# Gathers of the value stages paced two per chunk, their sums two chunks behind on VectorE, and the last mixer's exit to routing tile by tile

## The chip, the cores and the metric

The kernel runs on one core of a Trainium2 chip. The metric is device time in microseconds (us) of one execution, shown as the median of several runs. The engines are called as the profile calls them: PE is TensorE, DVE is VectorE, ACT is ScalarE, POOL is GpSimd, and SP is SyncE, which here only starts transfers.

## The reference, cut to what matters

A trunk of two layers runs over two groups of tokens: a prompt of 128 tokens (tag P) and a sample of 512 tokens (tag S), of 1024 features each, all in float32. Each layer is a mixer (layer 0: Fourier and short convolution; layer 1: an RG-LRU and an RWKV-7 recurrence) followed by PEER, a mixture over 16,384 experts of which each token takes 128 (8 heads of 16).

```
for each layer l:
    h = layer_norm(x) * (1 + sc1) + sh1
    x = layer_norm(ALPHA * x + g1 * (mixer(h) @ w_out))
    h2 = layer_norm(x) * (1 + sc2) + sh2
    # PEER: idx, gate = top 16 of the product keys, per head and token
    act = gelu(sum_d h2[t, d] * u[idx[t, k], d])
    ffn[t] = sum_k gate[t, k] * act[t, k] * v[idx[t, k]]
    x = layer_norm(ALPHA * x + g2 * ffn)
```

## The kernel before, in words

Tokens lie in tiles of 128. PEER is computed in two ways. For three of the four S tiles (`DENSE = (1, 2, 3)`) every expert is computed: `dense_peer` walks over 128 **chunks** of 128 experts. For a chunk, `hidden` multiplies the tokens by the chunk's slice of the table `u` (24 matmuls in a three-term split of float32, `split_matmul`), ACT applies gelu, DVE multiplies by the scattered gates (`ge * gt`, a **product**), ACT and DVE split it into `ah` and `al`, the chunk's slice of `v` is loaded and split into `vh` and `lw`, and 18 matmuls add it to the output. Half of the hidden tiles are computed earlier, in routing, and parked in DRAM (`spill`), so 64 chunks of a layer are light (18 matmuls) and 64 heavy (42). This walk is called the **value stage** here; there is one per layer.

For S tile 0 and for P, which are too small for that, the rows of `u` and `v` are **gathered**: `gather` starts an indirect DMA on POOL that brings one expert's row for each of 128 tokens, 128 x 4 KB, and one DVE instruction uses it (a **sum** below, be it a dot product with `h2` in `dots` or an addition to `acc` in `values`). There are 512 gathers a layer. They are **tasks**: generators in `B.tasks`, of which `B.pump(n)` takes the next n steps. `B.pump` is called from other work: `split` calls it `B.rate` times for each split table block (2 in routing, 0 in the value stage), `one_hot` once, the projections of layer 1's mixer through `B.pace`, and the value stage once per chunk with a share of what is left, `ceil(left / (122 - c))`. In layer 0 the last 88 tasks (`OVER`) are kept for the next mixer. A sum is held back until two more gathers were issued (`defer`, `use_gathered(2)`); gathered rows live in 4 buffers (`GW`), and in the value stage in `B.gb` = 3 more. Table blocks `w` have 3 buffers, and in a pool `B.wb` more.

A scheduler of the framework orders each engine's instructions by program order and by its own estimate of when each is ready; engines then run them strictly in that order. `pace(n, src)` puts a copy of one column of `src` on POOL and ties the next n gathers behind it, so that they start no sooner than `src` is written.

The mixer of layer 1 is a set of generators advanced in turn (`run` in `odd_mixers`): S's recurrence units, P's whole layer behind them, the LRU channels. When all are done, `peer_layer` opens with `end`, the **passage** to routing: the output projection of S (half of it, k = 0 to 3, was added before by `end_early`, so `self.early` is 4), residual, two layer norms, and the transposes into `hi` and `lo`, for two pairs of tiles, each pair loading its four `wout` blocks itself. Then `route` computes queries, scores and top 16, and `scatter_gates` the gates of the dense tiles; meanwhile gathers run.

## Time and profile before

| | us |
|---|---|
| median of 3 runs | 4570.66 |
| lowest and highest of them | 4562.15, 4586.86 |
| profiled execution | 4558.22 |
| its span, first to last instruction | 4556.4 |
| PE busy | 3837.5 (84%) |
| DVE busy | 3467.4 (76%) |
| POOL busy | 1387.9 (30%) |
| DMA moved | 1198 MB, 263 GB/s over the span |

The table's second part is from the profile page; the DMA engines' mean share and the granted PE clock are also given by stretch. A row of the view by stretches reads: start and end in us from the span's start, length, busy time of PE, PEld (weight loads), DVE, ACT and POOL with the number of instructions in brackets, granted PE clock as a share of 2.4 GHz, mean share of the 16 DMA engines, GB/s. The stretches used are: end of layer 0's routing (780 to 1024), layer 0's value stage (1024 to 1911, cut at 1545 where its gathers end), mixer of layer 1 (1911 to 2958), passage (2958 to 3088), routing of layer 1 (3088 to 3640), its value stage (3640 to 4532, cut at 4282 where the gathers end), and a tail of 24 us.

### The profile page before, as it was taken

Reading aid. Unit: us, or ns where it says so; the run is one execution under the profiler, and the core shown is the slowest. Engines: PE = TensorE matmul, PEld = TensorE weight load, DVE = VectorE, ACT = ScalarE, POOL = GpSimd, SP = SyncE. Lnnn points to the kernel's source line nnn. Section 1 sums busy time; section 2 is a strip of 40 time slices with the busy share of each in tenths; the row PEclk is TensorE's granted clock in tenths of the full one; section 3 lists DMA queues with packets and bytes.
Section 4 is the critical chain, followed back from the end, with each engine's and each line's share of the span. In section 5 each row is a group of like instructions: output and inputs, shape, how many; then the busy total and the mean of one; then the engine's idle time right before and its main releaser. Section 6 shows DMA issues by size and latency. Waiting matters only on the chain. (4 is left out here: it accounts for less than half of the span.)

```text
span 4556.4 us, 71571 instructions
## 1 busy us (share of the span) xinstructions
PE 3837.5 (84%) x26326; PEld 3142.3 (69%) x26326; DVE 3467.4 (76%) x7480; ACT 1757.4 (39%) x3391; POOL 1387.9 (30%) x1105
## 2 busy tenths in 40 slices
PE   7977968999888999778889877719779888988897
PEld 4653767997766788634665654508779877877786
DVE  3398999987889744668554786589999787888845
ACT  2211235763322333244575543203357623332332
POOL 0044322434556200044000232253125354466300
PEclk9997989999999999887888877759999999999999
DMA  9699856999999755368531566487569999999853
GB/s 342 227 350 356 264 196 236 349 357 355 360 360 362 280 175 172 128 237 286 177 101 58 182 222 205 169 289 248 171 225 341 346 367 342 346 365 369 310 170 120
DMA packets 455551, 1198.05 MB, mean 263 GB/s; under 512 B 52848, under 2 KB 195312, under 8 KB 452128
## 3 DMA queue, kind: packets, MB, share of 16 engines
q1 hardware_dynamic: 307744, 656.54, 41.4%
q0 software_dynamic: 147456, 536.94, 32.8%
q8 instruction: 207, 3.39, 0.3%
q14 instruction: 144, 1.18, 0.1%
HBM read 1093.34 MB, written 99.98 MB: 262 GB/s over the span
## 5 line engine op out<-in xcount | busy, mean ns | idle before, releaser
L1079 PE MATMUL ps<-hiS,lwS 128*128 128x384 f32 (+1 forms) x2304 | 817.5, 356 | 81.2 <-DVE lwS L1224 80.9
L1079 PE MATMUL ps<-loS,uhS 128*128 128x384 f32 (+1 forms) x2432 | 857.9, 353 | 1.1 <-DVE loS L432 1.1
L1079 PE MATMUL ps<-hiS,uhS 128*128 128x384 f32 (+1 forms) x2304 | 813.2, 353 | 51.3 <-ACT geS L1252 26.0
L1079 PEld LDWEIGHTS ps<-hiS,lwS 128*128 128x128 f32 x2304 | 447.2, 194 | 111.7 <-DVE lwS L1224 101.4
L1222 ACT ACTIVATE uhS<-w 128x1024 fp32r<-128x1024 f32 x304 | 320.8, 1055 | 527.3 <-PE ps L1079 358.6
L1285 PE MATMUL ps<-vh,ah 128*128 128x512 f32 x1536 | 429.4, 401 | 99.9 <-ACT vh L1222 78.8
L1152 POOL DMA_INDIRECT g<-v,idxP x256 | 351.7, 1374 | 515.8 <-DVE h2P L1168 311.9
L1152 POOL DMA_INDIRECT g<-u,idxS x256 | 349.0, 1363 | 512.9 <-DVE g L1138 391.9
L1079 PEld LDWEIGHTS ps<-hiS,uhS 128*128 128x128 f32 x2304 | 447.5, 194 | 82.3 <-ACT uhS L1222 34.1
L1285 PE MATMUL ps<-lwS,ah 128*128 128x512 f32 x1536 | 483.4, 396 | 10.9 <-DVE lwS L1224 10.8
L1079 PEld LDWEIGHTS ps<-loS,uhS 128*128 128x128 f32 x2432 | 471.5, 194 | 24.0 <-DVE loS L432 3.7
L1285 PE MATMUL ps<-vh,al 128*128 128x512 f32 x1536 | 477.3, 393 | 0.0
L1224 DVE TENSOR_TENSOR lwS<-w,uhS 128x1024 fp32r<-128x1024 f32 x304 | 369.7, 1217 | 122.9 <-ACT uhS L1222 82.0
L1152 POOL DMA_INDIRECT g<-v,idxS x256 | 367.8, 1437 | 237.6 <-DVE h2S L1168 178.6
L1224 DVE TENSOR_TENSOR lwS<-w,vh 128x1024 fp32r<-128x1024 f32 x256 | 312.9, 1223 | 153.7 <-issue 79.3
L1152 POOL DMA_INDIRECT g<-u,idxP x256 | 291.7, 1139 | 414.2 <-DVE g L1138 183.2
L1285 PEld LDWEIGHTS ps<-vh,ah 128*128 128x128 f32 x1536 | 289.1, 192 | 167.1 <-ACT vh L1222 92.5
L1278 ACT ACTIVATE ah<-geS 128x384 fp32r<-128x384 f32 x256 | 134.3, 525 | 671.4 <-PE ps L1285 598.9
L1138 DVE SCALAR_TENSOR_TENSOR g<-g,h2P 128x1024 f32<-128x1024 f32 x256 | 310.2, 1216 | 81.4 <-DMA g<-u,idxP 81.0
L1168 DVE SCALAR_TENSOR_TENSOR h2P<-g,wtP,h2P 128x1024 f32<-128x1024 f32 x254 | 324.6, 1278 | 50.7 <-DMA g<-v,idxP 49.2
L1285 PEld LDWEIGHTS ps<-lwS,ah 128*128 128x128 f32 x1536 | 291.2, 191 | 81.6 <-DVE lwS L1224 20.1
L1285 PEld LDWEIGHTS ps<-vh,al 128*128 128x128 f32 x1536 | 291.4, 190 | 62.8
(480 smaller groups left out, 6687.9 us busy)
## 6 DMA issues: line engine op xcount, KB each, us to landing
w<-ut SPq DMA_DIRECT2D x256, 512.0 KB
w<-v SPq DMA_DIRECT2D x256, 512.0 KB
w<-wblk SPq DMA_DIRECT2D x142, 512.0 KB
w<-wmod SPq DMA_DIRECT2D x96, 512.0 KB
gt<-G SPq DMA_DIRECT2D x64, 768.0 KB
w<-wout SPq DMA_DIRECT2D x56, 512.0 KB
ged<-geS SPq DMA_DIRECT2D x128, 192.0 KB
G<-fa SPq DMA_DIRECT2D x12, 2048.0 KB
```

Of the source, the lines that this page charges most:

```text
L1079: self.nc.tensor.matmul(out, a[:, s], b[:, k, :], start=k == 0 and i == 0, stop=k == 7 and i == 2)
L1138: self.nc.vector.scalar_tensor_tensor(u, u, 1.0, self.h2[t], OP.mult, OP.mult, accum_out=self.act[t][:, s:s + 1])
L1152: self.nc.gpsimd.indirect_dma_start(out=g, out_offset=None, in_=self.I[tab], in_offset=bass.IndirectOffsetOnAxis(ap=self.idx[t][:, s:s + 1 ...
L1168: nc.vector.scalar_tensor_tensor(acc, v, w[:, s:s + 1], acc, OP.mult, OP.add)
L1222: self.nc.scalar.activation(h, raw, AF.Copy)
L1224: self.nc.vector.tensor_tensor(lo, raw, h.bitcast(F32), op=OP.subtract)
L1278: nc.scalar.activation(ah, ge, AF.Copy)
L1285: nc.tensor.matmul(outs[n][h], a[:, s], b[:, 512 * h:512 * h + 512], start=c == 0 and i == 0, stop=c == 127 and i == 2)
```

## The change

In the value stage, each chunk now paces its gathers behind its own product: `pace(min(more, max(2, ceil(more / (122 - c)))), ge)`, so at least two per chunk as long as there are any. The sums are no longer released by the next gathers: `lag` is 5 there, and each chunk releases, behind its `al` on DVE, all gathers but those of the chunk before. Gathered rows get 4 more buffers instead of 3, table blocks 1 instead of 0. `B.rate` in routing is 1 instead of 2.

For a layer whose output projection was half done (`self.early`, layer 1's S), `end_tiles` replaces `end`: four `wout` blocks are loaded once, all four tiles are projected, and residual, norms and transposes run per tile, with 5 row buffers. In layer 1's mixer P's projections yield after each block, and P's first inputs are computed before its units are queued.

```diff
-        self.odd, self.tasks, self.pending, self.left = False, [], [], 0
+        self.odd, self.tasks, self.pending, self.left, self.lag = False, [], [], 0, 2
...
     def defer(self, *use):
         self.pending.append(use)
-        self.use_gathered(2)
-
-    def use_gathered(self, left=0):
-        while len(self.pending) > left:
-            f, *a = self.pending.pop(0)
-            with self.later(0):
+        self.use_gathered(self.lag)
+
+    def use_gathered(self, left=0, after=None):
+        with self.tc.issue_after(after.ins) if after else nullcontext():
+            while len(self.pending) > left:
+                f, *a = self.pending.pop(0)
                 f(*a)
 
     def pace(self, n, src):
-        if self.tasks:
+        if n and self.tasks:
...
+    def end_tiles(self, l, hT, lo):
+        nc, B = self.nc, self.B
+        ws = []
+        for k in range(self.early, 8):
+            w = B.rp.tile([128, D], F32, name=B.name("wo"), tag="wo", bufs=8 - self.early)
+            nc.sync.dma_start(w, self.I["wout"][l, k])
+            ws.append(w)
+        self.end_load(l)
...
+        for t in range(self.nt):
+            pts.append([self.pst(*(("pB", 2) if t == 3 else ())) for _ in range(2)])
+            for k in range(self.early, 8):
+                for h in range(2):
+                    nc.tensor.matmul(pts[t][h], self.yT[:, k, t * 128:(t + 1) * 128],
+                                     ws[k - self.early][:, 512 * h:512 * h + 512], start=k == self.early, stop=k == 7)
+        for t in range(self.nt):
...
+            self.residual(x, pts[t], g1, 1.0)
+            self.norm([x], g, b)
+            self.save(t, x)
+            self.norm([x])
+            self.transposed([x], (t,), mc, hT, lo)
...
@@ odd_lora
             lo.append(o)
+            yield
@@ wkv_inputs
                     self.shift(z[:, hp, :], z[:, hp, 1:T + 1], 4 * i + hp)
+                    if hp < 3:
+                        yield
@@ dense_peer
+        self.B.lag, fresh = 5, 0
         for c in range(128):
             if c == 127:
                 self.B.finish_task(first)
-            elif c < LAST:
-                more = self.B.left - (OVER if l < DEPTH - 1 else 0)
-                self.B.pump(max(0, -(-more // (LAST - c))))
...
             nc.scalar.activation(ah, ge, AF.Copy)
-            nc.vector.tensor_tensor(al, ge, ah.bitcast(F32), op=OP.subtract)
+            i = nc.vector.tensor_tensor(al, ge, ah.bitcast(F32), op=OP.subtract)
+            if self.B.lag > 2:
+                self.B.use_gathered(fresh, i)
+            had = len(self.B.pending)
+            if c < LAST:
+                more = self.B.left - (OVER if l < DEPTH - 1 else 0)
+                self.B.pace(min(more, max(2, -(-more // (LAST - c)))), ge)
+            fresh = max(0, len(self.B.pending) - had)
             vh, vl = self.split(self.dt, "vh", self.I["v"][l * NEXP + c * 128:l * NEXP + (c + 1) * 128])
@@ peer_layer
-                self.end(l, self.hi, self.lo, l == 0 and (lambda: B.modulation(1, 0)))
+                if self.early:
+                    self.end_tiles(l, self.hi, self.lo)
+                else:
+                    self.end(l, self.hi, self.lo, l == 0 and (lambda: B.modulation(1, 0)))
...
-                B.rate = 2
+                B.rate = 1
...
-                B.gp, B.gb, B.rp = self.dense_pool, 3, self.dense_pool
+                B.gp, B.gb, B.wb, B.rp = self.dense_pool, 4, 1, self.dense_pool
...
@@ prompt, in odd_mixers
-        P.odd_lora(l)
+        yield from P.odd_lora(l)
...
+        yield from P.wkv_inputs(l, P.inputs, 0)
```

How the change moves instructions is seen in three places. On POOL, in the middle of layer 0's value stage, stood bare gathers of `v` (`g` is a gathered row, `idxS` tile 0's expert numbers):

```order
L1152 DMA g_10465<-v,idxS_2899 128x1024
L1152 DMA g_10468<-v,idxS_2899 128x1024
L1152 DMA g_10502<-v,idxS_2899 128x1024
L1152 DMA g_10505<-v,idxS_2899 128x1024
L1152 DMA g_10539<-v,idxS_2899 128x1024
```

Now, on POOL at the same place (`pace` is the copy's target, `geS` a chunk's product):

```order
L225 COPY pace_12207<-geS_12009 128x1
L1197 DMA g_12209<-v,idxS_2899 128x1024
L1197 DMA g_12211<-v,idxS_2899 128x1024
L225 COPY pace_12277<-geS_12048 128x1
L1197 DMA g_12279<-v,idxS_2899 128x1024
L225 COPY pace_12347<-geS_12087 128x1
L1197 DMA g_12281<-v,idxS_2899 128x1024
```

A copy that waits for a chunk's product now stands ahead of that chunk's gathers.

On DVE, in the same stage (`h2S<-g` is a sum, `al` the low half of the product, `lwS<-w` the split of a table block, `geS` the product), before:

```order
L1168 SCALAR_TENSOR_TENSOR h2S_8844<-g_10465,wtS_8841,h2S_8844 128x1024
L1168 SCALAR_TENSOR_TENSOR h2S_8844<-g_10468,wtS_8841,h2S_8844 128x1024
L1168 SCALAR_TENSOR_TENSOR h2S_8844<-g_10502,wtS_8841,h2S_8844 128x1024
L1279 TENSOR_TENSOR al_10786<-geS_10508,ah_10785 128x384
L1224 TENSOR_TENSOR lwS_10687<-w_10683,uhS_10685 128x1024
L1168 SCALAR_TENSOR_TENSOR h2S_8844<-g_10505,wtS_8841,h2S_8844 128x1024
L1168 SCALAR_TENSOR_TENSOR h2S_8844<-g_10539,wtS_8841,h2S_8844 128x1024
L1224 TENSOR_TENSOR lwS_10725<-w_10721,vh_10723 128x1024
```

Now, on DVE at the same place; `geS_12048`, whose product started `g_12279` above, had its own `al` 14 rows ahead of this sum:

```order
L1269 TENSOR_TENSOR lwS_12357<-w_12353,vh_12355 128x1024
L1322 TENSOR_TENSOR al_12412<-geS_12126,ah_12411 128x384
L1213 SCALAR_TENSOR_TENSOR h2S_10590<-g_12279,wtS_10587,h2S_10590 128x1024
L1269 TENSOR_TENSOR lwS_12381<-w_12377,uhS_12379 128x1024
L1213 SCALAR_TENSOR_TENSOR h2S_10590<-g_12281,wtS_10587,h2S_10590 128x1024
L1319 TENSOR_TENSOR geS_12338<-geS_12338,gt_12447 128x384
L1269 TENSOR_TENSOR lwS_12427<-w_12423,vh_12425 128x1024
L1322 TENSOR_TENSOR al_12453<-geS_12198,ah_12452 128x384
```

The sums thin out to two per chunk and stand behind the `al` of two chunks later than the product that started their gathers. Counted over the stage, layer 0 had 213 sums, all in the first 70 chunks, and has 262 over 125 chunks; layer 1 had 256 in the first 94 and has 309, 189 of them in the first 64.

On DVE in layer 1's passage (`rsS` and the lines 401 to 407 are the small steps of a layer norm, `g<-g,h2P` a dot product with a row of `u`), before:

```order
L1138 SCALAR_TENSOR_TENSOR g_27517,actP_21590<-g_27517,h2P_21528 128x1024
L405 TENSOR_TENSOR rsS_26634<-rsS_26634 128x2
L1138 SCALAR_TENSOR_TENSOR g_27553,actP_21590<-g_27553,h2P_21528 128x1024
L406 SCALAR_TENSOR_TENSOR rsS_26634<-rsS_26634 128x2
L1138 SCALAR_TENSOR_TENSOR g_27556,actP_21590<-g_27556,h2P_21528 128x1024
L407 SCALAR_TENSOR_TENSOR rsS_26634<-rsS_26634 128x2
```

Now, on DVE in the passage (`h2P<-g` is a sum with a row of `v`):

```order
L1213 SCALAR_TENSOR_TENSOR h2P_29962<-g_30517,wtP_29959,h2P_29962 128x1024
L406 SCALAR_TENSOR_TENSOR rsS_26700<-rsS_26700 128x1
L406 SCALAR_TENSOR_TENSOR rsS_26775<-rsS_26775 128x1
L1213 SCALAR_TENSOR_TENSOR h2P_29962<-g_30555,wtP_29959,h2P_29962 128x1024
L407 SCALAR_TENSOR_TENSOR rsS_26700<-rsS_26700 128x1
L407 SCALAR_TENSOR_TENSOR rsS_26775<-rsS_26775 128x1
```

A sum still stands between the small steps, in which the second norm of one tile now goes with the first norm of the next. From the first residual to the last `loS` of the passage there were 52 sums and there are 74; from there to the value stage there were 108 and there are 13.

## Rows read from the trace of the kernel before

**Rows 1.** Busy time by stretch of the program, columns as explained above.

```profile
780.00:1024.00 244.00, 232.39 (x1512) 230.62 (x1510) 214.82 (x287) 174.63 (x417) 110.25 (x76) 0.99 0.95 351
1024.00:1545.00 521.00, 447.93 (x2028) 374.02 (x2029) 448.77 (x531) 150.90 (x205) 282.12 (x203) 0.97 0.97 359
1545.00:1911.00 366.00, 357.65 (x1726) 313.86 (x1724) 175.56 (x225) 129.37 (x174) 0.00 (x0) 0.99 0.52 166
1911.00:2958.00 1047.00, 835.59 (x11370) 570.77 (x11371) 703.23 (x2021) 488.48 (x1051) 222.75 (x251) 0.78 0.54 180
2958.00:3088.00 130.00, 34.77 (x109) 20.21 (x107) 112.08 (x208) 15.64 (x32) 69.17 (x58) 0.61 0.84 286
3088.00:3440.00 352.00, 302.80 (x1624) 275.73 (x1624) 346.90 (x1155) 160.27 (x335) 86.98 (x57) 0.95 0.64 215
3440.00:3640.00 200.00, 191.75 (x1262) 191.21 (x1260) 167.40 (x143) 142.12 (x349) 83.04 (x53) 0.99 0.96 354
3640.00:4282.00 642.00, 566.70 (x2568) 487.49 (x2569) 539.70 (x702) 192.75 (x259) 353.16 (x251) 0.94 0.98 358
4282.00:4532.00 250.00, 247.53 (x1178) 216.38 (x1176) 130.84 (x170) 86.99 (x116) 1.86 (x1) 0.99 0.52 170
```

**Rows 2.** PE's waits in 1024 to 1545: us in total, times, longest.

```profile
PE ps L1285 <- ACT vh L1222: 48.2, 23, 6.6
PE ps L1285 <- ACT ah L1278: 10.0, 1, 10.0
```

**Rows 3.** The chain that ended last: start, length, what (layer 1's value stage).

```profile
3816.83 4.12 PE ps L1285 x18
3820.95 4.18 PE ps L1079 x24
```

**Rows 4.** DMA of 1024 to 1545, of 1545 to 1911, and the page's spills.

```profile
DMA packets 78854, 186.80 MB, mean 359 GB/s; under 512 B 5892, under 2 KB 38513, under 8 KB 78824
...
g<-v,idxS POOLq DMA_INDIRECT x128, 8.3
...
DMA packets 35227, 60.90 MB, mean 166 GB/s; under 512 B 2044, under 2 KB 24060, under 8 KB 35205
...
ged<-geS SPq DMA_DIRECT2D x128, 192.0 KB
```

**Rows 5.** DVE's groups in 1024 to 1545: count, busy us, mean ns, idle before.

```profile
L1168 DVE SCALAR_TENSOR_TENSOR h2S<-g,wtS,h2S 128x1024 f32<-128x1024 f32 x127 | 162.8, 1282 | 1.8
L1224 DVE TENSOR_TENSOR lwS<-w,vh 128x1024 fp32r<-128x1024 f32 x67 | 81.6, 1220 | 12.1 <-ACT vh L1222 12.1
L1276 DVE TENSOR_TENSOR geS<-geS,gt 128x384 f32<-128x384 f32 x72 | 38.9, 553 | 41.3 <-DMA geS<-ged 21.9 <-ACT geS L1252 15.6 <-issue 3.5
```

**Rows 6.** POOL: pacing copies (ns, least/median/most), and gathers in 1024 to 1545.

```profile
L225 POOL COPY pace<-z x18: 174/287/1265, 201.5 to 2671.4; 128x1 f32<-128x1 f32 x18
...
L1152 POOL DMA_INDIRECT g<-v,idxS x128 | 179.2, 1400 | 127.8 <-DVE h2S L1168 93.1 <-DVE g L1138 16.3 <-issue 13.7
```

**Rows 7.** Timelines of PE and DVE in layer 1's passage.

```profile
2956.15 19.87 PE L502 MATMUL ps<-w,fa 128*128 128x512 f32 x40 [6.42 <-DMA w<-wout]
...
3074.38 3.34 PE L424 MATMUL ps<-cst,tmp 128*128 128x128 f32 x16 [70.08 <-DVE tmp L413]
...
2958.26 0.69 DVE L552 TENSOR_TENSOR half<-ps,row 128x512 f32<-128x512 f32 x1 [17.51 <-DMA w<-wout]
...
3055.57 0.17 DVE L403 TENSOR_SCALAR rsS<-rsS 128x2 int32<-128x2 int32 x1
```

**Rows 8.** DVE's sums in 2958 to 3088 (two rows) and 3088 to 3440.

```profile
L1138 DVE SCALAR_TENSOR_TENSOR g<-g,h2P 128x1024 f32<-128x1024 f32 x32 | 38.8, 1214 | 9.5 <-DMA g<-u,idxP 9.3
L1168 DVE SCALAR_TENSOR_TENSOR h2P<-g,wtP,h2P 128x1024 f32<-128x1024 f32 x19 | 24.4, 1284 | 7.2 <-DMA g<-v,idxP 7.1
...
L1168 DVE SCALAR_TENSOR_TENSOR h2P<-g,wtP,h2P 128x1024 f32<-128x1024 f32 x57 | 72.5, 1273 | 2.6 <-DMA g<-v,idxP 2.6
```

**Rows 9.** Layer 1's mixer while P's first projections run, by stretch.

```profile
2200.00:2240.00 40.00, 31.80 (x230) 29.33 (x231) 13.86 (x70) 14.49 (x37) 0.00 (x0) 0.83 0.63 194
```

More of the change, by code (lines that the diff above doesn't have):

```diff
@@ L375, in save, with row_of, mrow @@
         self.x[t] = d
-    def row_of(self, src):
-        o = self.B.wide("row", 3)
+    def row_of(self, src, bufs=3):
+        o = self.B.wide("row", bufs)
         self.nc.sync.dma_start(o, src.broadcast_to([128, D]))
         return o
-    def mrow(self, l, v):
-        return self.row_of(self.B.md[l, v][self.row:self.row + 1, :])
+    def mrow(self, l, v, bufs=3):
+        return self.row_of(self.B.md[l, v][self.row:self.row + 1, :], bufs)
     def mcols(self, l, v):
@@ L506, in end_project @@
         self.todo.append((grp, pts))
+    def end_tiles(self, l, hT, lo):
[6 more added lines that the diff above has]
+        self.end_load(l)
+        xs = []
+        for t in range(self.nt):
+            x = self.tmp()
+            nc.sync.dma_start(x, self.x[t])
+            xs.append(x)
+            if t == 1:
+                break
+        g1 = self.mrow(l, 2, 5)
+        g, b = self.row_of(self.I["lnaff"][l, 0:1], 5), self.row_of(self.I["lnaff"][l, 1:2], 5)
+        mc = self.mcols(l, 3)
+        self.h2, self.todo, pts = {}, None, []
+        for t in range(self.nt):
[4 more added lines that the diff above has]
+                                     ws[k - self.early][:, 512 * h:512 * h + 512], start=k == self.early, stop=k == 7)
+        for t in range(self.nt):
+            if t < len(xs):
+                x = xs[t]
+            else:
+                x = self.tmp()
+                nc.sync.dma_start(x, self.x[t])
+            self.residual(x, pts[t], g1, 1.0)
[3 more added lines that the diff above has]
+            self.transposed([x], (t,), mc, hT, lo)
+            if t not in self.dense:
+                sh2, sc2 = self.mrow(l, 3, 5), self.mrow(l, 4, 5)
+                h2 = self.h2[t] = self.keep([128, D], "h2")
+                nc.vector.scalar_tensor_tensor(h2, sc2, 1.0, x, OP.add, OP.mult)
+                nc.vector.tensor_tensor(h2, h2, sh2, op=OP.add)
     def end(self, *a):
@@ L1329, in peer_layer @@
             with B.tc.tile_pool(name=f"ends{l}", bufs=1, reuse_waits="tile") as B.rp:
-                self.end(l, self.hi, self.lo, l == 0 and (lambda: B.modulation(1, 0)))
+                if self.early:
+                    self.end_tiles(l, self.hi, self.lo)
+                else:
+                    self.end(l, self.hi, self.lo, l == 0 and (lambda: B.modulation(1, 0)))
             B.rp = None
@@ L1521, in odd_mixers @@
     B.odd_constants()
-    S.odd_lora(l)
+    for _ in S.odd_lora(l):
+        pass
     lru = [S.odd_lru(l, c) for c in range(4)]
```

2 lines of the change are left out of this document (1 added, 1 removed).

## The prediction

> **What bounds the kernel now.** I read the view by stretches first, since the shares of the whole span average stages with different limits. In layer 0's value stage up to 1545 us the DMA engines are busy 0.97 of the time at 359 GB/s while PE stands for 521 - 447.93 = 73 us; after 1545, when no gather is left, DMA falls to 0.52 and PE is busy 357.65 of 366 [rows 1]. Layer 1 repeats it: 0.98 at 358 GB/s with 642 - 566.70 = 75 us of idle PE, then 0.52 and a full PE [rows 1]. So one half of each value stage is bound by DMA and the other by PE. PE's waits name the same: 48.2 us for ACT's high half of a `v` block, which waits for its load, and 10.0 us once at the start [rows 2]. Three more places matter. In the passage PE is busy 34.77 of 130 us and DVE 112 of 130; in routing up to 3440 DVE is busy 346.90 of 352 with PE at 302.80; from 3440 PE is at 191.75 of 200 [rows 1]. So there the work of DVE, gather sums among it, sets the pace, and after it PE does. Layer 1's mixer has neither engine full (PE 836, DVE 703 of 1047 us) [rows 1]: chains of dependent steps.
>
> **The change, part by part.** *Layer 0's value stage.* A light chunk costs PE 4.12 us and a heavy one 4.18 more [rows 3]; 128 spills make 64 light chunks per layer [rows 4]. Measured, the stage's PE work is (447.93 + 357.65) / 128 = 6.29 us per chunk [rows 1]. A gather moves 128 x 4 KB = 0.524 MB. The stage moved 186.80 + 60.90 MB [rows 4], of which 203 gathers [rows 1] are 106.4, so loads alone are 141.3 / 128 = 1.10 MB per chunk. At 359 GB/s a chunk with two gathers takes 2.15 / 0.359 = 5.99 us of DMA, with three 2.68 / 0.359 = 7.45. Two fit under PE, three don't. Before, there were three per chunk in the first half and none in the second. After, there are 262 (49 more, taken from routing): `ceil(262 / 122)` is 3 until about chunk 18, then 2. Stall: 18 x (7.45 - 6.29) = 21 us, plus the 10.0 us of the start, which hangs on the scattered gates and stays. So 31 of the 73 us remain: **-42 us**. Bounds: -65 if only the start's wait stays, -10 if at 95% DMA load blocks of `v` still come late half as often.
>
> DVE there costs per chunk two sums of 1.28, one and a half splits of 1.22 and two operations of 0.55 [rows 5], together 5.5 us, under PE's 6.29. The 213 new pacing copies lie on POOL: a chunk's two gathers at 1.40 and a copy of 0.29 (median; 1.27 at most) [rows 6] are 3.1 us of 6.29. Copies and gathers at nothing, with PE as their cover.
>
> *Layer 1's value stage.* 53 more gathers come in, 309 in all: `ceil(309 / 122)` is 3 until about chunk 65. PE needs (566.70 + 247.53) / 128 = 6.36 us per chunk [rows 1]. Stall: 65 x (7.45 - 6.36) = 71 us, plus some 10 at the start. It had 75 + 2.5 idle [rows 1], so **0 us**: what pacing saves is paid for the 53 gathers. Bounds -30 (the fourth buffer of table blocks lets loads run ahead) to +12.
>
> On this term a rule of the Trainium skill speaks otherwise. The row has DMA 0.97 to 0.98 busy at 358 to 359 GB/s over 521 and 642 us [rows 1]. "DMA: Bandwidth & Descriptors", section "Bandwidth", gives 425 GB/s for a large transfer while the pair's other core is idle, and puts about 358 as the share when both stream. This program runs on one core, so by the page an estimate for three gathers is 2.68 / 0.425 = 6.3 us, and the stall of 71 us would be gone. The trace shows no room: the engines are full at 359. The sum keeps the row.
>
> *Layer 0's routing.* 49 sums leave it, at its end. There PE is busy 232 of 244 us [rows 1], so their DVE time was hidden: 0.
>
> *The passage.* Its end is DVE's: PE waits 70.08 us for the second pair's norm [rows 7]. The 52 sums there take 38.8 + 24.4 us and a little [rows 8]. Now 74 stand in the passage: 22 x 1.28 = +28. Norms by tile double the small steps: four tiles with two norms of 12 steps instead of two pairs, 48 more of some 0.17 [rows 7] = +8. Four `wout` loads fewer, and earlier: DVE waited 17.51 us for them [rows 7]; I take half, -8. Together **+28 us**, between 0 (the sums fill gaps in which DVE waits for DMA, 16.4 us [rows 8]) and +40.
>
> *Routing of layer 1.* Of 109 sums 13 are left. In the part where DVE is the bound, 57 [rows 8] become 13: 44 x 1.27 = 56 us less on DVE, which would put it at 291, under PE's 303. PE's idle time there is 352 - 302.80 = 49 us [rows 1], the most that can be gained. I take 35, since PE still waits for one-hots and for splits in between, and 2 more from the full part: **-37 us**, bounds -52 and -20.
>
> *Layer 1's mixer.* P's first projections stand in one block now, during which DVE is busy 13.86 of 40 us [rows 9] and S's recurrence stands still; they last some 60 us. Spread over S's units, part of that overlaps. Nothing in the trace prices it; the nearest rows bound it by the idle time of that block, -50, and by P's chain ending later, +25. I take **-10**, near zero, since PE is still 80% busy in that block [rows 9].
>
> Sum: -42 + 0 + 0 + 28 - 37 - 10 = -61 us. The profiled execution took 4558.2 us, 12 less than the median of the three runs; so 4497 against it, 4509 against the median. I put the forecast between them, **4500 us**.
>
> **The rivals.** *The passage eats the gain.* Gathers moved into the passage stand alternately with steps of a chain on which all queries wait. If DVE there also waits for each gather to land, +40, and routing gives only -20, the mixer nothing and the value stage -40, the sum is -20: 4540. For it: the 7.1 us and 9.3 us of such waits [rows 8]; against it: both stretches trade the same sums.
>
> *The mixer overlaps.* The interleaved projections hide fully: 45 instead of 10 us, 4465. For it stands DVE's low load there; against it, that P's routing then comes later beside S's last units.
>
> *DMA has headroom.* Layer 1's first 65 chunks run at PE's pace if the engines can move more than 359 GB/s: 71 us more, 4430. Against it is the 0.98 share. This is the case of the skill's page named above ("DMA: Bandwidth & Descriptors", section "Bandwidth").
>
> *VectorE waits in its row: slower.* A sum now has a fixed place between `al` and the split of `v`; if its rows aren't there, both halves of the next `v` block and so PE wait behind it. A gather needs 8.3 us from issue to landing [rows 4], and its chunk's second one 2 x 1.40 more of POOL [rows 6]: 11.1 us. If the sum truly comes two chunks after the gather's start, two light chunks give 8.24 us, and a light chunk stretches to 5.55, by 1.43 us. It hits 64 light chunks in layer 0 and 32 in layer 1's second half: 96 x 1.43 = 137, so 4630. It decides once the lead from issue to sum is under 11 us. Against it: products run ahead of their `al` by two to three chunks on DVE, and eight buffers allow four chunks of lead. Before, DVE waited 1.8 us in all ahead of these sums [rows 5].
>
> *No effect.* Gathers were spread before as far as the queues allow, and the scheduler's order in the routing gives back what the value stage wins: 4570.
>
> **How the numbers follow.** Chances: forecast 0.50, passage 0.20, mixer 0.12, headroom 0.04, VectorE waits 0.10, no effect 0.04. A measurement of this kernel can tell about 0.5% from no change, which is 4548 to 4593 around the median. The forecast, the mixer's and headroom cases are faster; of the passage case 0.12 is faster and 0.08 is within. So faster 0.78, same 0.12, slower 0.10. The range for 8 in 10: its low end is the headroom case with its 4430, also about the sum of the favourable bounds of the value stage and mixer; its high end 4580 takes in the passage case, no effect, and the unfavourable bounds. It leaves out the slower case.
>
> **What would show it.** In the profile after: layer 0's value stage from first to last chunk near 845 us instead of 887, DMA share level at 0.9 over all of it, PE idle about 31 us and that in the first 20 chunks; layer 1's value stage still in two parts, DMA full up to chunk 65; the passage from first residual to last transpose about 158 us instead of 130; routing behind it some 515 instead of 552, with DVE no longer full. Wrong would be: DVE waiting for gathers in the light chunks; a value stage of layer 1 that is much shorter than 880 us; a mixer that differs by over 40 us from its 1047.

## The result and the profile after

| | before | after |
|---|---|---|
| median, us | 4572.17 | 4503.23 |
| lowest and highest of 4 runs each | 4562.15, 4586.86 | 4492.41, 4510.93 |
| ratio, with its 95% interval | | 0.9845 [0.9811, 0.9879] |
| span of the profiled execution | 4556.4 | 4490.6 |

The changed kernel is 1.5% faster, and 4500 us had been forecast. The total hides that the parts came out otherwise, so the first thing to read is the view by stretches of the changed kernel (columns as in [rows 1]: start and end, length, busy PE, PEld, DVE, ACT, POOL with instruction counts, PE clock, DMA share, GB/s). The eight rows are layer 0's value stage in two parts, layer 1's mixer, the passage, routing in two parts, and layer 1's value stage in two parts.

```profile
1024.00:1440.00 416.00, 387.00 (x1808) 337.62 (x1809) 329.75 (x453) 135.42 (x184) 248.39 (x206) 0.96 0.96 347
1440.00:1849.00 409.00, 404.84 (x1944) 354.14 (x1943) 337.49 (x392) 143.40 (x195) 233.38 (x177) 1.00 0.90 323
1849.00:2930.00 1081.00, 851.00 (x11381) 570.71 (x11380) 740.06 (x2082) 490.94 (x1053) 249.86 (x246) 0.77 0.55 185
2930.00:3095.00 165.00, 29.54 (x88) 18.25 (x87) 140.57 (x276) 19.32 (x57) 87.74 (x73) 0.56 0.80 267
3095.00:3440.00 345.00, 320.67 (x1848) 297.10 (x1847) 315.81 (x1128) 189.24 (x417) 12.50 (x11) 0.99 0.52 174
3440.00:3612.00 172.00, 162.23 (x1054) 161.88 (x1053) 82.80 (x74) 113.49 (x268) 1.69 (x2) 0.98 0.60 207
3612.00:4060.00 448.00, 400.52 (x1827) 343.95 (x1827) 388.61 (x547) 135.09 (x184) 289.07 (x250) 0.95 1.01 376
4060.00:4466.00 406.00, 399.69 (x1918) 349.69 (x1917) 338.78 (x377) 140.32 (x191) 229.92 (x179) 1.00 0.90 326
```

Against [rows 1]: the DMA share of layer 0's value stage is level now (0.96 and 0.90 instead of 0.97 and 0.52), and PE's idle time there is 29 + 4 us instead of 73 + 8. Layer 1's value stage still begins full, at 1.01, but moves 376 GB/s where before it moved 358. The passage grew to 165 us, DVE is no longer full in routing (315.81 of 345 instead of 346.90 of 352), and the mixer grew.

The lengths below are taken the same way in every profiled execution: a value stage from its first to its last value matmul (L1285 before, L1335 after), the mixer from there to the first residual of the passage, the passage to its last transposed tile, routing to layer 1's first value matmul. All in us; the seven stretches of a row add up to its span, up to rounding. Each row is one execution, and runs of one kernel lie 6 to 45 us apart, so a few us in a stretch say nothing; each ratio is against runs of the kernel before taken beside that experiment. The experiments are told in the next two sections and are named there.

| kernel | ahead | value 0 | mixer | passage | routing | value 1 | tail | median, ratio to before |
|---|---|---|---|---|---|---|---|---|
| before | 1024 | 878 | 1056 | 131 | 555 | 888 | 25 | 4572 |
| after | 1026 | 823 | 1081 | 165 | 516 | 855 | 25 | 4503, 0.9845 [0.9811, 0.9879] |
| e1_value_only | 1036 | 846 | 1064 | 130 | 545 | 841 | 25 | 4486, 0.9816 [0.9791, 0.9841] |
| e8_buffers_only | 1036 | 840 | 1064 | 131 | 550 | 837 | 25 | 4479, 0.9789 [0.9763, 0.9815] |
| e11_table_only | 1031 | 812 | 1056 | 132 | 550 | 833 | 25 | 4438, 0.9712 [0.9681, 0.9743] |
| e12_rows_only | 1037 | 886 | 1067 | 130 | 553 | 887 | 25 | 4582, 1.0025 [1.0008, 1.0042] |
| e13_buffers_paced | 1051 | 826 | 1064 | 85 | 607 | 842 | 25 | 4499, 0.9837 [0.9803, 0.9871] |
| e5_old_buffers | 1031 | 844 | 1095 | 168 | 510 | 899 | 25 | 4560, 0.9967 [0.9946, 0.9989] |
| e6_even | 1025 | 821 | 1110 | 169 | 507 | 857 | 25 | 4512, 0.9862 [0.9836, 0.9887] |
| e7_sums_free | 1029 | 829 | 1079 | 170 | 511 | 862 | 25 | 4511, 0.9869 [0.9842, 0.9896] |
| e2_mixer_old | 1028 | 822 | 1100 | 171 | 516 | 845 | 25 | 4521, 0.9904 [0.9876, 0.9932] |
| e3_end_pairs | 1030 | 822 | 1060 | 131 | 550 | 850 | 25 | 4456, 0.9751 [0.9726, 0.9777] |
| e9_route_paced | 1029 | 818 | 1053 | 61 | 593 | 851 | 25 | 4429, 0.9699 [0.967, 0.9729] |
| e14_paced_two | 1036 | 819 | 1052 | 62 | 581 | 799 | 105 | 4457, 0.9755 [0.9719, 0.979] |

From before to after the stretches changed by -55, +25, +35, -39 and -33 us. The forecast had -42, -10, +28, -37 and 0. In the value stages not all of it is waiting: by the rows above and [rows 1], PE's busy time in layer 0's stage fell from 805.6 to 791.8 us for the same matmuls (3754 and 3752), and in layer 1's from 814.2 to 800.2. So about 41 of the 55 us and 19 of the 33 are idle time; why PE's own time fell isn't known.

PE's waits in layer 0's value stage, and then in layer 1's, in the changed kernel (us in total, times, longest):

```profile
PE ps L1124 <- ACT uhS L1267: 12.8, 5, 8.2
PE ps L1124 <- DVE lwS L1269: 11.1, 6, 4.5
PE ps L1335 <- ACT ah L1321: 8.0, 1, 8.0
PE ps L1335 <- ACT vh L1267: 4.3, 3, 1.6
...
PE ps L1124 <- ACT uhS L1267: 27.9, 16, 10.9
PE ps L1124 <- DVE lwS L1269: 18.0, 18, 3.8
PE ps L1335 <- ACT vh L1267: 17.6, 7, 9.8
```

In layer 0, the 48.2 us in 23 waits for a `v` block [rows 2] have become 4.3 in 3; the wait at the start (8.0, was 10.0) stays. In layer 1 PE still waits for tables, 63.5 us in these three rows.

### The profile page after: what moved, and what is told of

It reads as the page before. It is cut to its first block, busy times and chain, and to the rows that moved or that the text cites. A ratio compares the mean times of both kernels' runs of the same rounds, so it can differ in the third digit from the quotient of the medians.

```text
span 4490.6 us, 72172 instructions
## 1 busy us (share of the span) xinstructions
PE 3811.6 (85%) x26326; PEld 3127.6 (70%) x26326; DVE 3456.6 (77%) x7548; ACT 1758.5 (39%) x3418; POOL 1565.1 (35%) x1318
## 5 line engine op out<-in xcount | busy, mean ns | idle before, releaser
L1197 POOL DMA_INDIRECT g<-v,idxS x256 | 410.6, 1604 | 246.2 <-DVE h2S L1213 204.8
L1267 ACT ACTIVATE uhS<-w 128x1024 fp32r<-128x1024 f32 x304 | 320.0, 1053 | 430.6 <-PE ps L1124 330.1
L1335 PE MATMUL ps<-lwS,ah 128*128 128x512 f32 x1536 | 475.9, 391 | 1.3 <-DVE lwS L1269 1.3
L1335 PE MATMUL ps<-vh,al 128*128 128x512 f32 x1536 | 473.0, 390 | 0.0
L1335 PE MATMUL ps<-vh,ah 128*128 128x512 f32 x1536 | 413.5, 394 | 29.9 <-ACT vh L1267 21.9
L225 POOL COPY pace<-geS 128x1 f32<-128x1 f32 x244 | 154.1, 633 | 792.3 <-DVE geS L1319 758.0
L1197 POOL DMA_INDIRECT g<-v,idxP x256 | 330.7, 1292 | 228.7 <-DVE h2P L1213 123.7
L1335 PEld LDWEIGHTS ps<-vh,ah 128*128 128x128 f32 x1536 | 287.3, 189 | 86.2 <-ACT vh L1267 25.4
L1335 PEld LDWEIGHTS ps<-lwS,ah 128*128 128x128 f32 x1536 | 289.0, 188 | 62.8 <-DVE lwS L1269 2.2
```

The costliest lines, as they stand in the source:

```text
L225: self.pump(n, self.nc.gpsimd.tensor_copy(p, src[:, 0:1]))
L1197: self.nc.gpsimd.indirect_dma_start(out=g, out_offset=None, in_=self.I[tab], in_offset=bass.IndirectOffsetOnAxis(ap=self.idx[t][:, s:s + 1 ...
L1267: self.nc.scalar.activation(h, raw, AF.Copy)
L1335: nc.tensor.matmul(outs[n][h], a[:, s], b[:, 512 * h:512 * h + 512], start=c == 0 and i == 0, stop=c == 127 and i == 2)
```

## Experiments on the value stages

The theory at this point was the prediction's: the gathers, spread out, no longer push table loads beyond PE's pace. The value-stage part of the change also holds two buffers and a fixed place for the sums, so these were taken apart.

**The value stage's part alone (e1_value_only).** The kernel before with the edits in `pace`, `use_gathered`, `dense_peer` and the dense pool; mixer, passage and the rate in routing as before.

```diff
+            if self.B.lag > 2:
+                self.B.use_gathered(fresh, i)
...
+                self.B.pace(min(more, max(2, -(-more // (LAST - c)))), ge)
...
-                B.gp, B.gb, B.rp = self.dense_pool, 3, self.dense_pool
+                B.gp, B.gb, B.wb, B.rp = self.dense_pool, 4, 1, self.dense_pool
```

> The kernel before with the value-stage edits alone (pacing copies, sums two chunks behind, 4 and 1 more buffers); routing rate 2, passage in pairs and mixer as before. Theory, that a value stage is limited chunk by chunk by the larger of PE and its own DMA: with 213 gathers in layer 0 and 255 in layer 1, two a chunk nearly everywhere, layer 0's stage falls from 878 us to about 810 and layer 1's from 888 to about 825, the other stretches stay within 15 us, and the time is about 4440, below the changed kernel's 4503. Rival, that the stages only trade work with routing and the gain needs the lower routing rate: value stages near 823 and 854 as in the changed kernel, time about 4485 or more.

Measured 4485.5 us, ratio 0.9816 [0.9791, 0.9841]: this part alone gives at least as much as the whole change (0.9845 [0.9811, 0.9879], the intervals overlap), 32 us in layer 0's value stage and 47 in layer 1's. The theory's 4440 was not reached. The rival's number for the whole held, its stages of 823 and 854 us did not: 846 and 841. Which of the edits gives the gain, this run can't tell.

**The old buffers (e5_old_buffers).** The changed kernel with three more rows and no more table block, as before.

```diff
-                B.gp, B.gb, B.wb, B.rp = self.dense_pool, 4, 1, self.dense_pool
+                B.gp, B.gb, B.wb, B.rp = self.dense_pool, 3, 0, self.dense_pool
```

> The changed kernel with the old buffers in the value stages: 3 more gathered rows instead of 4, no more table block. Theory, that the buffers carry the faster DMA (layer 1's first 64 chunks moved at 376 GB/s instead of 358): that stretch falls back to about 360 GB/s and from 470 us to about 490, layer 1's stage from 854 to about 875, layer 0's from 823 to about 835, time about 4535. Rival, that the pacing alone does it: stages within 5 us of the changed kernel's, time 4500 to 4510.

Measured 4560.2 us, ratio 0.9967 [0.9946, 0.9989]. Without the buffers nearly the whole gain is gone: the theory held, and the loss was larger than its 835, 875 and 4535 us. Layer 0's stage is 844 us, so pacing alone took 34 us off 878 although 49 more gathers run in it. Layer 1's is 899, which is 11 more than before and 44 more than with the buffers. The first part of layer 1's stage moves 345 GB/s at a share of 0.94, where the changed kernel has 376 at 1.01. What came back is the wait for `v` blocks in that stage; in layer 0's it is 16.4 us, between the 48.2 of before and the 4.3 of after:

```profile
3648.00:4120.00 472.00, 397.78 (x1751) 333.60 (x1752) 374.23 (x528) 130.25 (x175) 290.23 (x242) 0.94 0.94 345
...
PE ps L1335 <- ACT vh L1267: 37.6, 12, 8.6
...
PE ps L1335 <- ACT vh L1267: 16.4, 8, 4.1
```

**The buffers alone (e8_buffers_only).** The kernel before with the eighth row and the fourth table block, and nothing else.

```diff
-                B.gp, B.gb, B.rp = self.dense_pool, 3, self.dense_pool
+                B.gp, B.gb, B.wb, B.rp = self.dense_pool, 4, 1, self.dense_pool
```

> The kernel before with the two buffer counts of the value stage alone (4 and 1 instead of 3 and 0). Theory, that without pacing more buffers only let the gathers run further ahead and still end early: stages within 15 us of 878 and 888, time 4560 to 4580. Rival, that the buffers are the gain: value stages near 846 and 841 as with all value-stage edits, time about 4490.

Measured 4479.5 us, ratio 0.9789 [0.9763, 0.9815]: the rival held. Two numbers in one line give as much as e1_value_only with its pacing, and no less than the whole change (its interval overlaps with both).

**One buffer each (e11_table_only, e12_rows_only).** The kernel before, with the table block or with the row.

```diff
-                B.gp, B.gb, B.rp = self.dense_pool, 3, self.dense_pool
+                B.gp, B.gb, B.wb, B.rp = self.dense_pool, 3, 1, self.dense_pool
```

```diff
-                B.gp, B.gb, B.rp = self.dense_pool, 3, self.dense_pool
+                B.gp, B.gb, B.rp = self.dense_pool, 4, self.dense_pool
```

> The kernel before with one more table block only (four instead of three), the row buffers as before. Theory: TensorE in the value stages waits for tables (vh 48.2 us x23, lwS among them), and a fourth block lets the next load start while three are held; so this carries nearly all of what both buffers gave: layer-0 value stage 840 to 850 (before 878), layer-1 839 to 852 (before 888), the median 4480 to 4500. Rival: the rows are what held the DMA back (GpSimd's gathers wait for a free row, and their late landing crowds the loads); then the stages stay within 10 us of before, 870 and 880, and the median is 4555 to 4575.

> The kernel before with one more gather row only (eight instead of seven), three table blocks as before. Theory (tables are what is short): the value stages stay within 10 us of before, 868 to 888 and 878 to 898, the median 4560 to 4585; a further gather in flight may even take bandwidth from the tables (+10). Rival (rows are short): both stages fall by 30 or more, to 845 and 850, and the median is near 4490.

The table block alone gives 4438.0 us, ratio 0.9712 [0.9681, 0.9743], and the row alone 4582.5, ratio 1.0025 [1.0008, 1.0042]. The theory of both runs held, and the table block gave more than it expected: 66 and 55 us in the two stages. The row brings nothing, and beside the table block it costs: 812 and 833 us without it, 840 and 837 with it. How much of these 28 us in layer 0 is the row and how much the scheduler's order isn't settled: e13_buffers_paced has the same buffers and its stage took 826.

How can a block help where the DMA engines were full? The same 400 us, 1040 to 1440, lie in layer 0's value stage in all three kernels. The DMA view of that window gives the total, the two queues (packets, MB, share of 16 engines: q1 holds the loads that SP starts, q0 the gathers) and the blocks of `v` loaded. Before:

```profile
DMA packets 60326, 142.90 MB, mean 357 GB/s; under 512 B 4513, under 2 KB 29473, under 8 KB 60303
q0 software_dynamic: 22884, 83.31, 55.2%
q1 hardware_dynamic: 37419, 59.30, 41.8%
...
w<-v SPq DMA_DIRECT2D x53, 512.0 KB
```

With the table block (e11_table_only):

```profile
DMA packets 64233, 146.10 MB, mean 365 GB/s; under 512 B 4638, under 2 KB 33182, under 8 KB 64208
q0 software_dynamic: 20755, 75.59, 50.5%
q1 hardware_dynamic: 43453, 70.19, 48.9%
...
w<-v SPq DMA_DIRECT2D x62, 512.0 KB
```

With the row (e12_rows_only):

```profile
DMA packets 61186, 146.15 MB, mean 365 GB/s; under 512 B 4616, under 2 KB 29536, under 8 KB 61163
q0 software_dynamic: 23797, 86.63, 57.2%
q1 hardware_dynamic: 37366, 59.23, 41.6%
...
w<-v SPq DMA_DIRECT2D x50, 512.0 KB
```

Both variants move 3 MB more than before, 365 instead of 357 GB/s. What differs is who gets it. The fourth block gives the loads 70.19 MB instead of 59.30 and takes 7.7 from the gathers: 62 chunks instead of 53. The eighth row gives the gathers 3.3 MB more, the loads nothing, and the stage falls back to 50 chunks. So the two streams share a full resource, and only the loads stand on PE's path: the gathers may run late, since in the second half of the stage DMA has time (0.52 [rows 1]). PE's waits for `v` blocks show the same, first with the table block over layer 0's stage, then with the row over 1024 to 1545:

```profile
PE ps L1285 <- ACT vh L1222: 13.1, 9, 1.5
```

```profile
PE ps L1285 <- ACT vh L1222: 41.7, 16, 7.2
```

What sets the shares is less clear. The obvious reading is that a stream gets the more the more transfers it may have open. But a buffer count also changes the order that the scheduler builds. Counted in DVE's row as it ran, the sums between layer 0's 16th and 64th `al` are 157 before, 120 with the block, 176 with the row and 131 with both (e8_buffers_only): 3.3, 2.5, 3.7 and 2.7 per chunk. A row buffer comes free only after its sum (before, POOL waits 157 of the 400 us above for such sums), so this order sets how many gathers go with each chunk. By the prediction's price, and at the rates above, an estimate for a chunk is then 7.9 us of DMA before, 6.6 with the block and 8.3 with the row, beside PE's 6.3. Over these 48 chunks the difference between 7.9 and 6.6 is some 60 of the 66 us. So the block alone may well have gained by spreading the gathers, which is what pacing was written to do, and these runs don't separate that from more open loads. Where the order is nearly the same, the buffers still count: after and e5_old_buffers have 100 and 97 such sums in layer 0 and 143 and 142 in layer 1, and the block and the row together are worth 21 and 44 us there.

With the block that stage is nearly PE's (e11_table_only, both halves): 394.68 of 409 and 393.55 of 403 us.

```profile
1031.00:1440.00 409.00, 394.68 (x1869) 343.15 (x1870) 347.15 (x410) 138.60 (x189) 198.95 (x147) 0.99 1.00 365
1440.00:1843.00 403.00, 393.55 (x1884) 342.57 (x1883) 264.39 (x326) 140.44 (x190) 85.10 (x56) 1.00 0.70 243
```

**Sums not tied (e7_sums_free).** The changed kernel with the sums released by the next gathers and not behind `al`.

```diff
-        self.B.lag, fresh = 5, 0
+        self.B.lag, fresh = 2, 0
```

> The changed kernel with pacing and buffers, but the sums released by the next two gathers as before and not tied behind al. Theory, that the sums' place hardly matters once the gathers are paced, since VectorE runs ahead: value stages within 8 us of 823 and 854, time 4500 to 4512. Rival, that a sum too early in the row makes VectorE wait for its rows and the splits of v behind it: DVE waits on gathers of over 30 us in the stages and 20 us or more lost in each, time 4540 or more.

Measured 4511.3 us, ratio 0.9869 [0.9842, 0.9896] beside 0.9845 [0.9811, 0.9879]: the intervals overlap, so tying the sums neither gains nor costs what a measurement can tell. In the changed kernel DVE stood idle 0.5 us ahead of its 127 `v` sums of layer 0 (columns: count, busy us, mean ns, idle before), so no sum there came too early for its rows:

```profile
L1213 DVE SCALAR_TENSOR_TENSOR h2S<-g,wtS,h2S 128x1024 f32<-128x1024 f32 x127 | 162.5, 1280 | 0.5
```

**An even share (e6_even).** The changed kernel with the gathers of layer 1 spread without a dense first half.

```diff
-                self.B.pace(min(more, max(2, -(-more // (LAST - c)))), ge)
+                self.B.pace(min(more, max(2, -(-more // (LAST - c)) if c % 2 == 0 else more // (LAST - c))), ge)
```

> The changed kernel with the count of gathers alternating between the rounded-up and rounded-down share, so that layer 1's 309 stand at 40 per 16 chunks instead of 48 and then 32. Theory, that three per chunk overload DMA and two leave it idle: at 2.5 per chunk (2.41 MB, 6.4 us at 376 GB/s) PE at 6.19 is hardly short, layer 1's stage falls from 854 us to about 825, time about 4475. Rival, that the total of bytes sets the stage: 299 MB at 376 GB/s are 796 us, below PE either way, and the stalls come from groups of light chunks, which stay: 845 to 855, time 4495 to 4510.

Measured 4512.2 us, ratio 0.9862 [0.9836, 0.9887]. The theory failed, the rival held: layer 1's stage is 857 us, as after (855). With the fourth block it doesn't matter whether three gathers a chunk stand in its first half or are spread over it. The total is 9 us above after's, with overlapping intervals; in the profiled execution the mixer took 1110 us instead of 1081, although no line of it differs. Why isn't known.

## Experiments on the mixer and the passage

**The mixer as before (e2_mixer_old).** The changed kernel without the yields in P's projections and without P's early inputs.

```diff
-        yield from P.odd_lora(l)
+        P.odd_lora(l)
...
-        yield from P.wkv_inputs(l, P.inputs, 0)
```

> The changed kernel with layer 1's mixer emitted as before (no yields between P's projections, no inputs ahead). Theory, that spreading P's projections pushed P's routing and its sums beside S's last recurrence units and lengthened the mixer: the stretch from the last value-stage matmul of layer 0 to the first residual returns from 1081 us to about 1056, time about 4478. Rival, that the 25 us come from the later gathers of layer 0's value stage or the later wout loads: the stretch stays at 1075 to 1085, time 4503.

Measured 4520.5 us, ratio 0.9904 [0.9876, 0.9932]. Neither number held: the mixer didn't return to 1056 us and didn't stay at 1081, it rose to 1100. So the mixer's edits are not what made it longer. That they save these 19 us isn't shown, since four kernels with the same lines in the mixer (after, e5, e6, e7) have 1079 to 1110.

**The passage in pairs (e3_end_pairs).** The changed kernel, with `end` in place of `end_tiles`.

```diff
-                if self.early:
+                if False:
```

> The changed kernel with the passage in pairs of tiles as before. Theory, that the passage only trades sums with routing: passage shorter by 25 to 35 us (165 to about 135), routing longer by about as much (516 to about 545), time 4500 to 4510. Rival, that the passage by tile is a loss by itself: passage 130 with routing still near 516, time about 4470.

Measured 4456.1 us, ratio 0.9751 [0.9726, 0.9777]. The theory that nothing but a trade of sums between passage and routing is at stake failed. The rival's 4470 was nearer, but not its reason, a routing that stays at 516: passage and routing together hold 681 us both here (131 + 550) and after (165 + 516), so that part is a trade. But the mixer fell from 1081 to 1060, which is most of the 23 us between the two profiled executions (the medians lie 47 apart). The mixer's last 100 us show why; before, then after:

```profile
2858.26:2958.26 100.00, 75.93 (x1107) 57.52 (x1105) 52.23 (x184) 21.37 (x51) 16.28 (x22) 0.67 0.47 161
```

```profile
2830.21:2930.21 100.00, 56.00 (x440) 38.06 (x437) 74.16 (x201) 17.43 (x31) 49.49 (x45) 0.58 0.86 297
```

DVE works 74.16 us there instead of 52.23, PE 56.00 instead of 75.93, and POOL starts gathers (49.49 instead of 16.28). Counted in the trace, 50 of P's sums stand in the mixer's last 120 us after, 20 before and 15 in e3_end_pairs. The other kernels agree: the five with the passage by tile and nothing to hold gathers back (after, e2, e5, e6, e7) have 46 to 54 such sums and a mixer of 1079 to 1110 us, the other nine 15 to 20 and 1052 to 1067. With the passage written by tile the scheduler drew P's sums forward, into the end of the recurrence. The timelines of the changed kernel show them between its steps (DVE, then PE; start, length, in brackets the idle time ahead and its releaser):

```profile
2885.30 0.21 DVE L1054 TENSOR_TENSOR wst<-ps,l 128x64 f32<-128x64 f32 x1
2885.43 1.22 DVE L1183 SCALAR_TENSOR_TENSOR g<-g,h2P 128x1024 f32<-128x1024 f32 x1
...
2887.12 1.21 DVE L1183 SCALAR_TENSOR_TENSOR g<-g,h2P 128x1024 f32<-128x1024 f32 x1
...
2888.25 0.22 DVE L1054 TENSOR_TENSOR wst<-ps,l 128x64 f32<-128x64 f32 x1
...
2885.57 0.48 PE L1053 MATMUL ps<-wst,l 64*64 64x64 f32 x4 [3.66 <-DVE wst L1054]
2888.53 0.48 PE L1053 MATMUL ps<-wst,l 64*64 64x64 f32 x4 [2.48 <-DVE wst L1054]
...
2913.56 30.10 PE L531 MATMUL ps<-wo,fa 128*128 128x512 f32 x64 [13.99 <-DMA wo<-wout]
```

A step of the state (`wst`) on DVE takes 0.21 us and its matmuls 0.48, yet they come 3 us apart, with one or two sums of 1.2 us in between; in all nine kernels without the early sums the last steps are 0.8 to 0.9 us apart. The gathers, started early, may also crowd the loads: PE waits 13.99 us for `wout` before the passage's projection, where [rows 7] has 6.42.

**The sums of routing held back (e9_route_paced).** The changed kernel; gathers that are started between the blocks of S's routing wait for the block that is being split, so their sums can't be drawn forward.

```diff
-        self.B.pump(self.B.rate)
+        if self.B.rate:
+            self.B.pace(self.B.rate, raw)
```

> The changed kernel with the gathers of S's routing tied behind the table block that is being split, so that the 62 sums of v rows leave the passage and stand in routing (20 in the passage, 122 in routing). Theory, that DVE's sums stretch the passage while PE waits: passage from 165 us to about 105 (54 sums of 1.28 less), routing from 516 to about 550 since PE has only 24 us of slack there, time about 4475. Rival, that DVE's total sets both stretches: their sum stays at 681 within 10 us, time 4503.

Measured 4429.4 us, ratio 0.9699 [0.967, 0.9729]: the theory's direction, and 46 us more than it expected. The mixer is 1053 us, the passage 61. Passage, first part and second part of routing:

```profile
2900.00:2961.00 61.00, 27.43 (x88) 16.78 (x87) 55.77 (x193) 17.21 (x56) 2.83 (x4) 0.69 0.22 78
2961.00:3250.00 289.00, 238.68 (x1196) 212.70 (x1194) 266.20 (x1008) 109.14 (x218) 87.01 (x85) 0.92 0.61 201
3250.00:3554.00 304.00, 277.46 (x1708) 272.81 (x1709) 260.72 (x356) 192.44 (x467) 160.90 (x122) 0.95 0.86 312
```

Two sums are left in the passage instead of 74. PE's waits for its norms fell from 133.9 to 33.6 us in all (four waits each), and those for a step of the state from 15.9 to 5.9 (after, then e9_route_paced):

```profile
PE ps L424 <- DVE tmp L413: 133.9, 4, 38.2
PE ps L1053 <- DVE wst L1054: 15.9, 5, 4.9
```

```profile
PE ps L424 <- DVE tmp L413: 33.6, 4, 11.6
...
PE ps L1053 <- DVE wst L1054: 5.9, 4, 4.0
```

The 121 sums stand in routing now, which takes 593 us instead of 516, but passage and routing together are 654 instead of 681. Neither PE nor DVE is full in routing's two parts (238.68 and 266.20 of 289), so the sums fill gaps there that the passage does not have.

**The same edit in pairs (e13_buffers_paced).** e8_buffers_only with the edit of e9_route_paced.

> The kernel before with both buffers and with the gathers between the blocks of the routing issued on GpSimd behind the block that is being split; no pacing in the value stages, no passage by tiles, the mixer as before. Theory: the value stages are those of the buffers alone (840, 837), and the passage with routing becomes shorter by as much as it did in the changed kernel with the same edit (passage and routing there from 681 to 654, 27 us), so the median is 4450 to 4465. Rival: the edit pays only where the passage goes by tiles, since there the gathers' sums were queued in VectorE's row between the norms; in pairs it moves time between passage and routing and nothing is gained: 4475 to 4490.

Measured 4498.9 us, ratio 0.9837 [0.9803, 0.9871]: neither number held, and the rival was the nearer. Passage and routing together are 692 us, 11 more than in e8_buffers_only, and the part ahead, in which layer 0's routing lies, is 15 longer. Holding gathers back pays beside the passage by tiles and not in this kernel. Its passage goes in pairs, and it starts two gathers at a block instead of one; which of the two matters, this run can't tell.

**Five blocks and seven rows (e14_paced_two).** e9_route_paced with a table block in place of a row.

```diff
-                B.gp, B.gb, B.wb, B.rp = self.dense_pool, 4, 1, self.dense_pool
+                B.gp, B.gb, B.wb, B.rp = self.dense_pool, 3, 2, self.dense_pool
```

> The changed kernel with the gathers between the routing's blocks issued behind the block being split, and with five table blocks and seven rows in place of four and eight (the same memory). Theory: a table block is worth more than a row, and two gathers a chunk need no eighth row; the value stages fall by a further 5 to 15 us each (818 to 808, 851 to 840), the median is 4400 to 4420. Rival: four blocks are enough to keep the loads ahead, and the lost row delays the gathers whose sums stand five behind: the stages stay or rise by up to 15 us each, the median is 4425 to 4460.

Measured 4457.4 us, ratio 0.9755 [0.9719, 0.979]. Half of the theory held: layer 1's stage fell to 799 us, 52 below e9_route_paced and far more than the 5 to 15 expected, while layer 0's stayed (819). But the tail behind layer 1's grew from 25 to 105, so that the total lies where the rival had it, for another reason. The stage's two halves and the 71 us behind it:

```profile
3550.00:3950.00 400.00, 387.16 (x1834) 338.44 (x1835) 325.88 (x432) 134.29 (x184) 205.91 (x194) 0.98 0.97 352
3950.00:4349.00 399.00, 396.54 (x1908) 348.06 (x1907) 337.94 (x421) 140.47 (x191) 216.76 (x192) 1.00 0.94 343
4349.00:4420.00 71.00, 0.65 (x3) 0.19 (x1) 69.10 (x57) 0.00 (x0) 47.62 (x47) 0.54 0.93 360
```

PE is through at 4349, idle only 15 us of 799. Then 47 gathers are still to be started and 56 sums to be done (DVE's timeline: 73.93 us of them at a stretch), since POOL waits for free rows, which DVE's sums release (waits of POOL in the stage):

```profile
4343.81 73.93 DVE L1213 SCALAR_TENSOR_TENSOR h2S<-g,wtS,h2S 128x1024 f32<-128x1024 f32 x56
...
POOL g L1197 <- DVE g L1183: 146.7, 89, 4.2
POOL g L1197 <- DVE h2S L1213: 86.7, 59, 3.7
POOL g L1197 <- DVE h2P L1213: 68.2, 41, 5.8
```

The gathers, so far hidden, became the end of the kernel. This is the other side of e11_table_only: what the loads gain, the gathers lose, and with 309 of them in the stage there is no slack left to lose. Here too it stands in the order: between the 16th and the 64th `al` of layer 1 DVE's row has 101 sums instead of 145 in e9_route_paced, and 50 behind the last one.

## Why the prediction was right in sum, and where not

**Layer 0's value stage: -42 forecast, -55 measured, the reading half right.** The DMA share was level as said (0.96, 0.90), and within the stage PE's idle time fell to the 31 us that had been forecast, some 20 of them in the first 20 chunks. The rest of the 55 is PE's own time, which the sum held at 6.29 us a chunk and which came out at 6.19. But the 31 us took the buffers, too. Pacing by itself gives 34 us (e5_old_buffers against before); the other 21 are the buffers (after against e5_old_buffers), which the sum had at nothing here. And the pacing edit isn't needed for the gain: the table block alone gives 66, and may do it by the same spreading.

**Layer 1's value stage: 0 forecast, -33 measured, 3 us outside the bound of -30.** It is the sum of +11 for pacing with 53 more gathers (e5_old_buffers) and -44 for the buffers. The step that failed is the price of a chunk with three gathers, "2.68 / 0.359 = 7.45": it took the rate that stood in [rows 1] with the DMA full for the most that DMA gives, and the table block for a bound at the side. The stall counted from it, 71 us of the first 65 chunks, measured 47 in the first 448 us; with the 376 GB/s of that stretch the same sum gives 65 x (2.68 / 0.376 - 6.36) = 50. The waits of [rows 2], 23 of them for the same thing, could have been read as the sign of a missing buffer. The Trainium skill, "Perfetto Trace Analysis", section "Optimization Strategy", says that a gap which keeps coming back on the engine that should be saturated can mean too little room for the next tile, buffer count among the reasons. The traces agree where the order is the same: with the two buffers the waits for `v` fell from 16.4 to 4.3 us in layer 0 and from 37.6 to 17.6 in layer 1. A missing buffer was not all of it, since pacing alone had taken layer 0's from 48.2 to 16.4.

**The rival that DMA has headroom** was put at 0.04 against "the engines are full at 359". The rate rose to 376 GB/s at a share of 1.01 (layer 1's first half, after), so the full share was no ceiling, and by the mechanism this rival was nearer the truth than the forecast. Its 71 us of stall were not all given back: 47 remained. The Trainium skill, "DMA: Bandwidth & Descriptors", section "Bandwidth", gives 425 GB/s for a large transfer while the pair's other core is idle, and about 358 as the share when both stream. None of the stretches shown here reached the 425, and the 376 is above the 358.

**Passage and routing: +28 and -37 forecast, +35 and -39 measured, right.** The sums in the passage (74 were forecast, 73 are in this view of DVE over 2930 to 3095) and the norms by tile account for it:

```profile
L1213 DVE SCALAR_TENSOR_TENSOR h2P<-g,wtP,h2P 128x1024 f32<-128x1024 f32 x61 | 78.2, 1282 | 21.2 <-DMA g<-v,idxP 21.2
L1183 DVE SCALAR_TENSOR_TENSOR g<-g,h2P 128x1024 f32<-128x1024 f32 x12 | 14.7, 1226 | 2.1 <-DMA g<-u,idxP 2.1
```

That is 92.9 us of sums where [rows 8] has 63.2, and 23.3 us of waiting for gathers instead of 16.7. What the forecast left out is that none of it had to be there: without the sums the passage takes 61 us (e9_route_paced).

**The mixer: -10 forecast, +25 measured, wrong in sign.** It was costed by its own edits, and these do little: with them and without the early sums the mixer takes 1060, 1053 and 1052 us (e3, e9, e14), without either 1056 to 1067 (before, e1, e8, e11, e12, e13). The loss came from the next stage: P's sums, drawn forward into the recurrence's end. That step is missing from the prediction. The step "P's chain ending later, +25" has the size, but not the cause.

**VectorE waiting in its row** (0.10) didn't happen: sums waited 0.5 us in layer 0, and untying them changed nothing that can be told.

So that 4500 came so near 4503 is luck: the errors cancel, 13 and 33 us too little gain in the value stages against 35 and 7 too little loss in mixer and passage.

The fastest of these kernels are e9_route_paced, 4429 us (0.9699 [0.967, 0.9729]), and e11_table_only, 4438 us (0.9712 [0.9681, 0.9743]); their intervals overlap. The one is the change with one more edit, the other the kernel before with one more table block. The two together, that is e9_route_paced with the old seven rows and four blocks, were not tried. Open stay the mixer's 29 us in e6_even, the row's exact price in layer 0, PE's shorter own time in the value stages, and how much of the lone table block's gain is the order and how much the open loads.

## What to carry to other kernels

Where two streams share a full DMA, count the buffers of each before counting bytes: try the next buffer for the stream that the critical engine waits for, and check that the other still ends in time. Where a scheduler sets the order, a buffer count changes that too, so count the transfers per step in the trace before calling the gain one of depth. Repeated short waits for the same load can be a sign of a missing buffer even where the DMA share says "full". When a stage is rewritten in finer steps, look at what the scheduler draws forward into the dependent chain ahead of it, and hold those instructions back with a wait on something that comes late enough.

## What had not been expected of the hardware

A DMA share of 0.97 to 0.98 was not the most that the engines move: 358 to 359 GB/s before, 365 in layer 0 with one more block or one more row, 376 in layer 1 after, each with the share at about 1.0. So a share at its end didn't say what the engines could still move. With nearly the same order of gathers, two more buffers took the first part of layer 1's stage from 345 GB/s at 0.94 to 376 at 1.01; what in the mix of transfers sets the rate isn't shown.
